# Rewriting the head statistics of an mLSTM stage, with a fourth raw weight tile and another order of loads and exponentials, in a two-layer streaming encoder

## The chip, the cores and the metric

The kernel runs on 1 core of a Trainium2 chip (trn2). The time is device microseconds of one execution on that core, the median of three runs. Besides, one execution was taken by the hardware profiler; every view of a profile below comes from that one. The engines are called PE (TensorE's matmuls; PEld is its weight loads), DVE (VectorE), ACT (ScalarE), POOL (GpSimd) and SP (SyncE, which only issues transfers here).

## The reference, cut to what matters

The program is an encoder trunk of two layers over 512 tokens of width 1024, in f32. Layer 0 mixes with 4 mLSTM heads of width 192 and 4 heads of attention to 256 memory tokens; layer 1 mixes with 12 heads of band attention and again memory attention. Each layer ends in a gated MLP with a causal convolution. What the change touches is the mLSTM head and what is done to its result:

```python
num = einsum('bhts,bhse->bhte', s, vv) + inter[..., None] * einsum('bhtd,bhde->bhte', qq, c_st)
den = sum(s, axis=-1) + inter * einsum('bhtd,bhd->bht', qq, n_st)
h = num / maximum(abs(den), exp(-m_t))[..., None]
...
hm = hm * rsqrt(mean(hm * hm, axis=-1, keepdims=True) + EPS)      # per head, 192 wide
mix_out = hm * a_head_g * sigmoid(o)
x = x + concatenate([mix_out, mem_out], axis=-1) @ w_out
```

The division by the bounded denominator and the norm of a head's row are one scale per token and head: with q = max(den², exp(-2 m)), the row `num` is multiplied by 1 / sqrt(mean(num²) + EPS q). Both versions of the kernel compute that.

## The kernel before

All activations lie transposed: 128 channels on the partitions, 512 tokens along the row. An f32 matrix is split into a rounded part and a rest, and a product is three matmuls (`mm3`, L167 to L171). A raw weight tile comes by SP's queue into one of three `wr` buffers (`load`), and ACT and DVE split it into `wh` and `wl` (`parts`, L130 and L131). `project` is one tile of 128 outputs over 8 such steps, with a yield behind each.

Order: a planner places the instructions on each engine by the order in which they are written and by its own estimate of when they are ready. The written order comes from generators: `weave(job, filler, each)` takes `each` steps of the filler for every yield of the job, and a yield of a number counts for that many. `pin` puts an instruction behind the one written before it on its engine. In the stage of this case the jobs are `mlstm_head(0)` to `mlstm_head(3)` and two rounds of memory attention, and the fillers are projections (query, key, gate and memory query tiles: `a_tiles`, `a_memory_queries`) and, later, parts of the output projection (`OutProjection.part`, which accumulates groups of output tiles over the input tiles that are there already; `finish` does the remaining output tiles whole and feeds the next norm).

A head: `weighted_scores(s)` for the four key tiles (an exponential of a row that POOL has spread over the partitions, L1155; a triangular mask on POOL, L1157; the scores in a PSUM bank, L164 and L519; their product on DVE, L1166; its split by ACT and DVE into `pt`), `products(s)` (two PSUM tiles `nums`, which hold 192 value channels, and the row sums spread over the 64 partitions that are left), then the statistics: both tiles squared on ACT (L1193) and multiplied by the output gate on DVE (L1195), and for each of four token tiles two f32 matmuls with the constants `mcf` as moving operand, which sum the squares of the numerator in one column and the mean of the squared denominators in the other:

```python
nc.tensor.matmul(st[:, 2 * T : 2 * T + 2], sqs[0][:, sl], mcf[:, 0, :], start=True, stop=False)
nc.tensor.matmul(st[:, 2 * T : 2 * T + 2], sqs[1][:, sl], mcf[:, 1 + odd, :], start=False, stop=True)
yield 0.581
```

The denominators are bounded from below by `floor2`, an exponential of the running maxima `mr`, which eight small transposes bring, with `acol`, to token-major columns (L1096 to L1099). Then come a reciprocal root by Newton's steps (`rsqrt`), two diagonal matrices (`diagonal`) and a matmul with ones (`spread`, L244) that brings the scale back along the rows, and the gated rows are scaled and split (L1214 to L1217) for the output projection. The memory's keys and values (`load_memory_kv`) come through a `wr` buffer. Buffers that matter: `u`, 57 tiles of 128x512; `bias`, 4 tiles for the spread exponents, asked for `NEXT` = 4 ahead; PSUM banks `mm` 3, `sc` 3, `tr` 2.

Of the kernel before, what the change touches and what calls it, by code (L numbers as in the profile page):

```python
# [55 lines left out]
def trunk(  # L56
# [25 lines left out]
    bufs = {"wr": 3, "wh": 3, "wl": 3, "u": 57, "t": 8, "pt": 2, "s": 16, "rb": 3, "bias": 4}  # L82
# [32 lines left out]

    mcf = cpool.tile([P, 3, 2], F32, name="mcf")
    V.memset(mcf, 0.0)
    V.memset(mcf[:, 0, 0:1], 1.0)
    V.memset(mcf[:HD, 1, 0:1], 1.0)
    V.memset(mcf[HD:, 1, 1:2], 1.0 / HD)  # L120
    V.memset(mcf[:HD, 2, 1:2], 1.0 / HD)
    V.memset(mcf[HD:, 2, 0:1], 1.0)

# [49 lines left out]
    def project(w, c0, act, tag="mm"):  # L173


        n = len(act)
        wh, wl = weights(rows(w, c0, P), n, P)
        o = ps(tag)
        for k in range(n):
            mm3(o, wh[:, k, :], wl[:, k, :], act[k][0], act[k][1], k == 0, k == n - 1)  # L180
            yield
        return o
# [374 lines left out]
    def memory_attention(q, kv, hp, mixes):  # L557
# [7 lines left out]
        def softmax(T2):  # L565
# [5 lines left out]
            for h in range(2):  # L571
# [3 lines left out]
                for i in range(2):  # L575
                    A.activation(e[:, i, :], ss[h][:, i, :], AF.Exp, bias=mx[:, i : i + 1], accum_out=sm[:, i : i + 1])
# [30 lines left out]
    class OutProjection:  # L607
# [19 lines left out]
        def finish(self, gnames):  # L627
            logarithms()
            norm = Norm()
            acts = [[] for _ in gnames]  # L630
            for j in range(KT):
                o = self.o[j] if j in self.o else run(project(self.w, j * P, self.mixes))
# [382 lines left out]
    floor2 = cpool.tile([P, TT, AH], F32, name="floor2")  # L1015
    NEXT = 4
# [14 lines left out]
    def gate_rows():  # L1031
# [19 lines left out]
        lfr, br, ar, mr = (sb("t", [P, S])[:AH, :] for _ in range(4))  # L1051
# [43 lines left out]
        for T in range(TT):  # L1095
            nc.tensor.transpose(tp[:, T * AH : (T + 1) * AH], ar[:, T * P : (T + 1) * P], ident[:AH, :AH])  # L1096
            nc.tensor.transpose(tp[:, 16 + T * AH : 16 + (T + 1) * AH], mr[:, T * P : (T + 1) * P], ident[:AH, :AH])
        pin(V.tensor_copy(acol, tp[:, :16].rearrange("p (t h) -> p t h", t=TT)))
        A.activation(floor2, tp[:, 16:32].rearrange("p (t h) -> p t h", t=TT), AF.Exp, scale=-2.0)  # L1099
# [3 lines left out]
    def qk_tile(c):  # L1103
# [8 lines left out]
        A.activation(acc, acc, AF.Silu)  # L1112
# [31 lines left out]
    def mlstm_head(h):  # L1144
# [6 lines left out]
        def weighted_scores(s):  # L1151
# [3 lines left out]
            A.activation(e[:, :n], spreads.pop((h, s)), AF.Exp, bias=acol[:, s, h : h + 1])  # L1155
# [34 lines left out]
        sqs = []  # L1190
        for o, j, r in ((nums[0], full, slice(0, P)), (nums[1], sh, rs)):
            sq = sb("t", [P, S])
            A.activation(sq, o, AF.Square)  # L1193
            sqs.append(sq)
            V.tensor_tensor(out=og[j][r, :], in0=o[r, :], in1=og[j][r, :], op=ALU.mult)  # L1195
        yield
        st = ps("sc")
        for T in range(TT):
            sl = slice(T * P, (T + 1) * P)
            nc.tensor.matmul(st[:, 2 * T : 2 * T + 2], sqs[0][:, sl], mcf[:, 0, :], start=True, stop=False)  # L1200
            nc.tensor.matmul(st[:, 2 * T : 2 * T + 2], sqs[1][:, sl], mcf[:, 1 + odd, :], start=False, stop=True)
            yield 0.581
        st = st[:, : 2 * TT].rearrange("p (t c) -> p t c", c=2)
        z, fc = small(), small()
        V.tensor_tensor(out=z, in0=st[:, :, 1], in1=floor2[:, :, h], op=ALU.max)
        V.tensor_scalar(z, z, EPS, 1e-35, op0=ALU.mult, op1=ALU.max)
        V.scalar_tensor_tensor(z, st[:, :, 0], 1.0 / DH, z, op0=ALU.mult, op1=ALU.add)
        rsqrt(fc, z)
        dg = diagonal(fc)
        yield 2.673  # L1210
# [8 lines left out]
    outp = OutProjection(a_w_out, mixes, (0, 3, "mm"), (3, 5, "tr"))  # L1219
# [5 lines left out]
    run(fill)  # L1225
    fill = chain(a_tiles(2), a_memory_queries(0), a_tiles(3, 4), a_tiles(5), a_memory_queries(1))
    memkv = load_memory_kv(0)
    weave(mlstm_head(0), fill, 1.4)
    until(lambda: og[2] is not None, fill)
    weave(mlstm_head(1), fill, 1.125)  # L1230
# [11 lines left out]
    fill = chain(fill, outp.part(1, 0, 1, 2, 6), outp.part(1, 3, 7))  # L1242
    weave(job, fill, 0.862)
    run(chain(fill, outp.part(0, 4, 5), outp.part(1, 4, 5)))
# [278 lines left out]
```

## Time and profile before

| | |
|---|---|
| median of 3 runs | 1194.93 us (1194.7 to 1196.32) |
| profiled execution | 1195.72 us |
| its span, first to last instruction | 1194.0 us |
| mean granted TensorE clock | 0.999 |
| PE busy | 1183.5 us (99%) |
| DVE busy | 961.7 us (81%) |
| ACT busy | 725.2 us (61%) |
| POOL busy | 130.3 us (11%) |
| head stage, about | 100 to 255 us of the span |

In a timeline row stand the start and the duration in us, the engine, the line of the kernel, the operation, output<-inputs by the program's names, the shapes and, in brackets, the idle time before it with what ended it. Matmuls overlap, so the time one takes of the engine is read from its start to the next one's. A row of a group has the busy time in us and the mean duration in ns behind the bar. A row of the waits has the sum in us, the number and the longest. A row of a window has its length and the busy time (and count) of PE, PEld, DVE, ACT and POOL, the granted clock, the DMA engines' share and GB/s. "f32" on PE stands for split operands too; an unsplit f32 matmul shows as two passes.

### The profile page before, as it was taken

The numbers are of one execution on the slowest core, as the hardware profiler recorded it, in microseconds if no ns is written. First come the engines' busy times: TensorE is split into PE (matmuls) and PEld (weight loads), VectorE is DVE, ScalarE is ACT, GpSimd is POOL, SyncE is SP. The second block draws the span as 40 slices with busy tenths as digits, with TensorE's granted clock in tenths as the row PEclk, the third lists the DMA queues.
The fourth block names the chain that finished last, engine by engine and source line by source line (L and its number), as shares of the span: only waits on it lengthen the run. The fifth ranks groups of instructions, "written<-read, shape, count | busy, mean of one in ns | idle before, by whom it ended". The sixth has DMA issues, their size and how long they took to land.

```text
span 1194.0 us, 18184 instructions
## 1 busy us (share of the span) xinstructions
PE 1183.5 (99%) x6719; PEld 1037.0 (87%) x6719; DVE 961.7 (81%) x1760; ACT 725.2 (61%) x1294; POOL 130.3 (11%) x222
## 2 busy tenths in 40 slices
PE   9999999999999999999999999999999999999997
PEld 9988888888899998999888888888889988999986
DVE  6877788788978888888698888997896888888855
ACT  5648677655656555555576677776565655555545
POOL 1211201010021111111020000101001011011100
PEclk9999999999999999999999999999999999999999
DMA  8645313444265676665464313246336455665551
GB/s 289 212 108 140 84 54 80 152 144 141 88 156 147 156 165 165 154 144 123 142 204 123 89 54 101 69 135 185 111 99 141 116 139 135 142 141 139 119 158 71
DMA packets 200155, 158.61 MB, mean 133 GB/s; under 512 B 8344, under 2 KB 179838, under 8 KB 200066
## 3 DMA queue, kind: packets, MB, share of 16 engines
q1 hardware_dynamic: 183906, 119.74, 34.1%
q0 software_dynamic: 15584, 36.67, 14.9%
q8 instruction: 53, 0.87, 0.3%
q10 hardware_dynamic: 576, 1.05, 0.2%
q14 instruction: 36, 0.29, 0.1%
HBM read 128.89 MB, written 32.46 MB: 135 GB/s over the span
## 4 chain that ended last, share of the span: by engine, by line
PE 92%; ACT 3%; DVE 2%; DMA 1%; SPq 1%; issue 0%; POOL 0%; POOLq 0%; DVEq 0%; ACTq 0%
PE pmm L169 15%; PE pmm L170 15%; PE pmm L171 15%; PE ptr L171 6%; PE ptr L169 6%; PE ptr L170 6%; PE pmm L785 6%; PE psc L171 5%; PE psc L170 5%; PE psc L169 5%; PE pmm L784 3%; PE psc L519 2%; PE ptr L1350 1%; DMA wr<-in_mem_w_kv_dram 1%; PE ptr L1371 1%; PE ptr L1372 1%
## 5 line engine op out<-in xcount | busy, mean ns | idle before, releaser
L169 PE MATMUL pmm<-u,wh 128*128 128x512 f32 (+1 forms) x872 | 309.1, 355 | 0.3 <-ACT u L130 0.2
L170 PE MATMUL pmm<-u,wh 128*128 128x512 f32 (+1 forms) x872 | 306.2, 351 | 0.0
L171 PE MATMUL pmm<-u,wl 128*128 128x512 f32 (+1 forms) x872 | 306.0, 351 | 0.0
L131 DVE TENSOR_TENSOR wl<-wr,wh 128x1024 fp32r<-128x1024 f32 (+3 forms) x172 | 199.8, 1163 | 57.0 <-ACT wh L130 55.0
L130 ACT CAST wh<-wr 128x1024 fp32r<-128x1024 f32 (+3 forms) x172 | 172.4, 1004 | 97.7 <-PE pmm L170 44.5
L171 PEld LDWEIGHTS pmm<-u,wl 128*128 128x128 f32 x872 | 164.5, 189 | 21.1
L169 PEld LDWEIGHTS pmm<-u,wh 128*128 128x128 f32 x872 | 164.5, 189 | 18.5 <-ACT u L130 1.1
L170 PEld LDWEIGHTS pmm<-u,wh 128*128 128x128 f32 x872 | 164.7, 189 | 18.2 <-DVE u L131 0.5
L169 PE MATMUL ptr<-u,wh 128*128 128x512 f32 x272 | 106.7, 392 | 0.0
L171 PE MATMUL ptr<-u,wl 128*128 128x512 f32 x272 | 106.1, 390 | 0.0
L753 POOL DMA_DIRECT2D xspill<-t x64 | 55.6, 869 | 461.1 <-ACT t L752 450.4
L170 PE MATMUL ptr<-u,wh 128*128 128x512 f32 x272 | 105.9, 389 | 0.0
L130 ACT CAST u<-pt 128x512 fp32r<-128x512 f32 x102 | 63.0, 620 | 46.8 <-DVE pt L875 46.7
L131 DVE TENSOR_TENSOR u<-pt,u 128x512 fp32r<-128x512 f32 x102 | 69.9, 688 | 11.2 <-ACT u L130 8.5
L169 PE MATMUL psc<-u,wh 128*128 128x256 f32 (+1 forms) x232 | 76.1, 328 | 0.0
L171 PE MATMUL psc<-u,wl 128*128 128x256 f32 (+1 forms) x232 | 75.9, 327 | 0.0
L170 PE MATMUL psc<-u,wh 128*128 128x256 f32 (+1 forms) x232 | 75.9, 327 | 0.0
L937 ACT ACTIVATE t<-t 128x512 f32<-128x512 f32 x34 | 21.6, 634 | 79.3 <-DVE t L660 79.3
L785 PE MATMUL pmm<-u,u 128*128 128x512 f32 x192 | 69.6, 397 | 0.0
L821 DVE TENSOR_TENSOR t<-t,pmm 128x256 f32<-128x256 f32 x72 | 30.2, 419 | 44.9 <-ACT t L819 44.8
L752 ACT COPY t<-ptr 128x512 f32<-128x512 f32 x64 | 37.4, 585 | 43.1 <-PE ptr L171 43.1
L660 DVE SCALAR_TENSOR_TENSOR t<-t,cols,t 128x511 f32<-128x511 f32 x80 | 59.7, 746 | 3.7 <-ACT t L667 3.7
(300 smaller groups left out, 2673.8 us busy)
## 6 DMA issues: line engine op xcount, KB each, us to landing
wr<-in_ffn_w_up_dram SPq DMA_DIRECT2D x54, 512.0 KB, 4.2
wr<-in_ffn_w_down_dram SPq DMA_DIRECT2D x38, 512.0 KB, 4.1
pt<-in_ffn_w_up_dram SPq DMA_DIRECT2D x34, 512.0 KB, 6.2
xspill<-t POOLq DMA_DIRECT2D x64, 256.0 KB, 5.2
wr<-in_a_w_in_dram SPq DMA_DIRECT2D x20, 512.0 KB, 3.7
xspill<-u POOLq DMA_DIRECT2D x32, 256.0 KB, 2.6
u<-xspill SPq DMA_DIRECT2D x32, 256.0 KB, 5.0
wr<-in_w_kv_dram SPq DMA_DIRECT2D x12, 512.0 KB, 3.7
```

Of the source, the lines that this page charges most:

```text
L130: high = A.copy(hi, src) if on_act else V.tensor_copy(hi, src)
L131: low = V.tensor_tensor(out=lo, in0=src, in1=f(hi), op=ALU.subtract)
L169: nc.tensor.matmul(o, lh, rh, start=first, stop=False, skip_group_check=more)
L170: nc.tensor.matmul(o, lh, rl, start=False, stop=False, skip_group_check=more)
L171: nc.tensor.matmul(o, ll, rh, start=False, stop=last, skip_group_check=more)
L519: nc.tensor.matmul(o, a, b, start=first and i == 0, stop=i == 1)
L660: V.scalar_tensor_tensor(acc[:, n:], src[:, : S - n], self.fw[:, c * FT + j : c * FT + j + 1], acc[:, n:], op0=ALU.mult, op1=ALU.add,)
L752: A.copy(t, o)
L753: G.dma_start(xspill[j], t, accum_op=ALU.add)
L784: nc.tensor.matmul(r[:, :H], w[1][:, k], p[i - 1][:, :H], start=False, stop=False, skip_group_check=True)
L785: nc.tensor.matmul(r, w[0][:, k], p[i - 1], start=False, stop=k == n - 1, skip_group_check=True)
L821: V.tensor_tensor(out=o, in0=o, in1=r[:, H:], op=ALU.add)
```

## The change

- The two squared tiles are combined before they are summed. The rows of the second tile that hold squared denominators are scaled and bounded by floors in one DVE operation, then both tiles are added (`tensor_add`), and one f32 matmul with a column of ones per token tile sums them, four per head. `mcf` and its six memsets go. The gate's multiplications are written behind the squares. The due times in the tail of a head become 3.6 and 5.
- The floors are rows now: `floor_rows` takes the exponential of `mr` (4 rows of 512), scales and bounds it, stores it in DRAM and loads each row back over 64 partitions, into two `u` tiles that live until the heads 1 and 3 have used them. Four of the eight small transposes go.
- `wr` has 4 buffers, `bias` 3, and `NEXT` is 3.
- `load_memory_kv(0)` is written behind head 0.
- The Silus of the query and key tiles, the exponentials of the heads' scores and those of memory attention (in both layers) are pinned.
- Output tile 5 becomes a third group of the first output projection, in an `sc` bank, whose parts over the inputs 0, 1, 2, 3, 6 and 7 are written into head 3's filler; `finish` (in both layers) loads and splits the weights of the first two tiles that remain before the norm's work.

```diff
-    bufs = {"wr": 3, "wh": 3, "wl": 3, "u": 57, "t": 8, "pt": 2, "s": 16, "rb": 3, "bias": 4}
+    bufs = {"wr": 4, "wh": 3, "wl": 3, "u": 57, "t": 8, "pt": 2, "s": 16, "rb": 3, "bias": 3}
...
-    mcf = cpool.tile([P, 3, 2], F32, name="mcf")
-    V.memset(mcf, 0.0)
...
-    def project(w, c0, act, tag="mm"):
+    def project(w, c0, act, tag="mm", ready=None):
...
-        wh, wl = weights(rows(w, c0, P), n, P)
+        wh, wl = ready or weights(rows(w, c0, P), n, P)
...
-                    A.activation(e[:, i, :], ss[h][:, i, :], AF.Exp, bias=mx[:, i : i + 1], accum_out=sm[:, i : i + 1])
+                    pin(
+                        A.activation(
+                            e[:, i, :], ss[h][:, i, :], AF.Exp, bias=mx[:, i : i + 1], accum_out=sm[:, i : i + 1]
+                        )
+                    )
...
             logarithms()
+            rest = [j for j in range(KT) if j not in self.o]
+            ready = {j: weights(rows(self.w, j * P, P), KT, P) for j in rest[:2]}
...
-                o = self.o[j] if j in self.o else run(project(self.w, j * P, self.mixes))
+                o = self.o[j] if j in self.o else run(project(self.w, j * P, self.mixes, ready=ready.get(j)))
...
-    floor2 = cpool.tile([P, TT, AH], F32, name="floor2")
-    NEXT = 4
+    floor2 = dram.tile([AH, S], F32, name="floor2")
+    floors = []
+    NEXT = 3
...
-        lfr, br, ar, mr = (sb("t", [P, S])[:AH, :] for _ in range(4))
+        lfr, br, ar = (sb("t", [P, S])[:AH, :] for _ in range(3))
+        mr = sb("rb", [P, S])[:AH, :]
+        floors.append(mr)
...
-            nc.tensor.transpose(tp[:, 16 + T * AH : 16 + (T + 1) * AH], mr[:, T * P : (T + 1) * P], ident[:AH, :AH])
         pin(V.tensor_copy(acol, tp[:, :16].rearrange("p (t h) -> p t h", t=TT)))
-        A.activation(floor2, tp[:, 16:32].rearrange("p (t h) -> p t h", t=TT), AF.Exp, scale=-2.0)
+
+    def floor_rows():
+        mr = floors.pop()
+        pin(A.activation(mr, mr, AF.Exp, scale=-2.0))
+        V.tensor_scalar(mr, mr, EPS * DH / HD, 1e-35, op0=ALU.mult, op1=ALU.max)
+        G.dma_start(floor2, mr)
+        for hp in range(2):
+            floors.append(sb("u", [P, S]))
+            for odd, half in enumerate(reversed(HEADS)):
+                row = floor2[2 * hp + odd]
+                src = bass.AP(tensor=row.tensor, offset=row.offset, ap=[[0, HD], [1, S]])
+                G.dma_start(floors[hp][half, :], src)
...
-        A.activation(acc, acc, AF.Silu)
+        pin(A.activation(acc, acc, AF.Silu))
...
-            A.activation(e[:, :n], spreads.pop((h, s)), AF.Exp, bias=acol[:, s, h : h + 1])
+            pin(A.activation(e[:, :n], spreads.pop((h, s)), AF.Exp, bias=acol[:, s, h : h + 1]))
...
         sqs = []
+        for o in reversed(nums):
+            sqs.insert(0, sb("t", [P, S]))
+            A.activation(sqs[0], o, AF.Square)
+        dr = HEADS[1 - odd]
+        V.scalar_tensor_tensor(
+            sqs[1][dr, :], sqs[1][dr, :], EPS * DH / HD, floors[hp][dr, :], op0=ALU.mult, op1=ALU.max
+        )
+        V.tensor_add(sqs[0], sqs[0], sqs[1])
         for o, j, r in ((nums[0], full, slice(0, P)), (nums[1], sh, rs)):
-            sq = sb("t", [P, S])
-            A.activation(sq, o, AF.Square)
-            sqs.append(sq)
             V.tensor_tensor(out=og[j][r, :], in0=o[r, :], in1=og[j][r, :], op=ALU.mult)
         yield
+        yield 3.6
         st = ps("sc")
         for T in range(TT):
-            sl = slice(T * P, (T + 1) * P)
-            nc.tensor.matmul(st[:, 2 * T : 2 * T + 2], sqs[0][:, sl], mcf[:, 0, :], start=True, stop=False)
-            nc.tensor.matmul(st[:, 2 * T : 2 * T + 2], sqs[1][:, sl], mcf[:, 1 + odd, :], start=False, stop=True)
-            yield 0.581
-        st = st[:, : 2 * TT].rearrange("p (t c) -> p t c", c=2)
+            nc.tensor.matmul(st[:, T : T + 1], sqs[0][:, T * P : (T + 1) * P], ones[:, :1], start=True, stop=True)
         z, fc = small(), small()
-        V.tensor_tensor(out=z, in0=st[:, :, 1], in1=floor2[:, :, h], op=ALU.max)
-        V.tensor_scalar(z, z, EPS, 1e-35, op0=ALU.mult, op1=ALU.max)
-        V.scalar_tensor_tensor(z, st[:, :, 0], 1.0 / DH, z, op0=ALU.mult, op1=ALU.add)
+        V.tensor_scalar(z, st[:, :TT], 1.0 / DH, None, op0=ALU.mult)
         rsqrt(fc, z)
         dg = diagonal(fc)
-        yield 2.673
+        yield 5
         fb = spread(dg, "sc")
...
-    outp = OutProjection(a_w_out, mixes, (0, 3, "mm"), (3, 5, "tr"))
+    outp = OutProjection(a_w_out, mixes, (0, 3, "mm"), (3, 5, "tr"), (5, 6, "sc"))
...
+    floor_rows()
     fill = chain(a_tiles(2), a_memory_queries(0), a_tiles(3, 4), a_tiles(5), a_memory_queries(1))
-    memkv = load_memory_kv(0)
     weave(mlstm_head(0), fill, 1.4)
     until(lambda: og[2] is not None, fill)
+    memkv = load_memory_kv(0)
...
-    fill = chain(fill, outp.part(1, 0, 1, 2, 6), outp.part(1, 3, 7))
+    fill = chain(fill, outp.part(2, 0, 1, 2, 3, 6, 7), outp.part(1, 0, 1, 2, 6), outp.part(1, 3, 7))
     weave(job, fill, 0.862)
-    run(chain(fill, outp.part(0, 4, 5), outp.part(1, 4, 5)))
+    run(chain(fill, outp.part(0, 4, 5), outp.part(1, 4, 5), outp.part(2, 4, 5)))
```

More of the change, by code (lines that the diff above doesn't have):

```diff
@@ L114, in trunk @@
     V.memset(eps, EPS)
-    mcf = cpool.tile([P, 3, 2], F32, name="mcf")
[L117 to L122, printed above, removed]
     HEADS = (slice(0, HD), slice(HD, P))
```

## The prediction

> **What bounds the kernel now.** I read the page first, then the waits of TensorE (PE), then the timeline of each engine through the stage of the four mLSTM heads, and last the table by windows. The page and the waits:
>
> ```profile
> span 1194.0 us, 18184 instructions
> PE 1183.5 (99%) x6719; PEld 1037.0 (87%) x6719; DVE 961.7 (81%) x1760; ACT 725.2 (61%) x1294; POOL 130.3 (11%) x222
> PE 92%; ACT 3%; DVE 2%; DMA 1%; SPq 1%; issue 0%; POOL 0%; POOLq 0%; DVEq 0%; ACTq 0%
> ...
> PE pmm L428 <- DVE mcf L117: 1.1, 1, 1.1
> PE ptr L392 <- ACT cols L320: 0.9, 1, 0.9
> PE ptr L588 <- DVE t L579: 0.3, 1, 0.3
> ```
>
> PE is busy for 1183.5 of 1194.0 us, 92% of the chain that ends last runs on it, and its longest visible wait after the start is 0.3 us. A transfer or another engine that gets faster therefore gives nothing by itself; what is taken out of PE's stream counts in full, if the stream stays dense. Busy time hides two things, though. Matmuls overlap, so a price has to be read from start to start; and a stall shorter than a matmul's tail shows only as a start that comes late. The timeline of PE around the statistics of head 0 shows the pace:
>
> ```profile
> 120.16 0.40 PE L170 MATMUL pmm<-u,wh 128*128 128x512 f32 x1
> 120.39 0.39 PE L171 MATMUL pmm<-u,wl 128*128 128x512 f32 x1
> 120.62 0.40 PE L169 MATMUL pmm<-u,wh 128*128 128x512 f32 x1
> ...
> 125.21 0.28 PE L1200 MATMUL psc<-mcf,t 128*128 128x2 f32 x2
> 125.35 0.36 PE L1201 MATMUL psc<-mcf,t 128*128 128x2 f32 x2
> 125.57 0.36 PE L1200 MATMUL psc<-mcf,t 128*128 128x2 f32 x2
> 125.80 0.36 PE L1201 MATMUL psc<-mcf,t 128*128 128x2 f32 x2
> 126.02 0.47 PE L169 MATMUL pmm<-u,wh 128*128 128x512 f32 x1
> 126.33 0.39 PE L170 MATMUL pmm<-u,wh 128*128 128x512 f32 x1
> ```
>
> A 512-column matmul takes 0.23 us (120.16, 120.39, 120.62). A statistics matmul moves two columns and still takes 0.11 us a pass: two passes from 125.57 to 125.80, and eight, two token tiles, 0.81 us from 125.21 to 126.02. The 512-column matmul behind such a burst is followed after 0.31 us (126.02 to 126.33), 0.08 us late.
>
> **The f32 sum (the largest term).** The groups by line, over the head stage:
>
> ```profile
> L1201 PE MATMUL psc<-mcf,t 128*128 128x2 f32 x32 | 5.8, 251 | 0.0
> L1200 PE MATMUL psc<-mcf,t 128*128 128x2 f32 x32 | 4.9, 222 | 0.0
> ```
>
> The 64 passes are 4 heads x 4 token tiles x 2 matmuls x 2 passes. By the rows above, the 16 tiles cost 8 x 0.81 = 6.5 us. In the timeline they stand in about three bursts a head with fill between, 12 in all, so 12 x 0.08 = 1.0 us of late starts come on top; and the first pair of a burst takes 0.14 us (125.21 to 125.35) instead of 0.23, which four bursts more than eight save, 0.4. Together 7.1 us. The new kernel has one matmul of one column per tile, 8 passes a head; that is the 0.81 us of the burst from 125.21 plus one late start, 0.9 us, and 3.6 us for four heads. Gain: 7.1 - 3.6 = **3.5 us**. Bounds: 0 if a new tile costs as much as the old pair; 7.1 - 4 x 0.81 + 4 x 0.14 = 4.4 if the new passes too are parted by fill and nothing behind them starts late. I take 3.5, since the row is of the same form but for a column. The Trainium skill (TensorE: Matmul & The Clock Gate, Back-to-back issue gap) gives 81 ns a matmul for a sustained stream of weight load and matmul at 128 columns; by that the 32 passes would be worth 2.6 us and the time 0.9 us more. The row has 0.11 us, and the measurement decides.
>
> **Floors as rows.** Four of eight transposes go:
>
> ```profile
> 88.35 0.22 PE L1096 MATMUL ptr<-ident,t 4*128 4x4 f32 x1
> ...
> 88.81 0.20 PE L1097 MATMUL ptr<-ident,t 4*128 4x4 f32 x1
> 88.94 0.50 PE L169 MATMUL pmm<-u,wh 128*128 128x512 f32 x1
> ```
>
> Eight take 0.59 us (88.35 to 88.94), so four less give **0.3 us**. In exchange POOL gets one store and four broadcasts; its own broadcasts take 0.55 us each, and it idles 14.22 us ahead of the first of head 0:
>
> ```profile
> 100.53 0.55 POOL L1029 DMA_DIRECT2D bias<-exponents  x1 [14.22 <-ACT t L1155]
> 106.75 0.58 ACT L1126 ACTIVATE u<-pmm 128x512 f32<-128x512 f32 x1
> ```
>
> That is 5 x 0.55 = 2.8 us of issue, plus the landing of the store. They are read only ahead of head 0's statistics (125.21), some 17 us behind the gate at 106.75 after which the floors' exponential runs, so I cost it at nothing; without that cover head 0's mask would come some 3 to 5 us late (it stands on POOL behind them).
>
> **Squares and DVE.** Each head loses two small operations (0.16 us each) and gains a 64-row and a 128-row pass over 512 columns:
>
> ```profile
> L1195 DVE TENSOR_TENSOR u<-ptr,u 128x512 f32<-128x512 f32 (+1 forms) x8 | 5.4, 686 | 5.0 <-ACT t L1193 4.9
> L539 DVE TENSOR_TENSOR t<-ptr,t 64x512 f32<-64x512 f32 x4 | 2.7, 682 | 0.8 <-ACT t L538 0.8
> L1205 DVE TENSOR_TENSOR s<-psc,floor 128x4 f32<-128x4 f32 x4 | 0.7, 163 | 2.6 <-PE psc L1201 2.6
> 160.00:190.00 30.00, 29.92 (x145) 24.68 (x144) 24.88 (x44) 27.45 (x48) 0.66 (x2) 1.00 0.22 64
> ```
>
> 0.68 + 0.69 - 2 x 0.16 = 1.05 us a head, 4.2 us in all. In the fullest window of the stage (last row: PE, weight loads, DVE, ACT) DVE has 24.88 of 30 us, so 1.05 fits; and the longer due times (3.6 and 5 instead of 0.581 each and 2.673) leave the planner more projections to put beside it. Cost 0, bounds 0 to 4.2. The multiplications by the output gate now follow the squares instead of standing between them.
>
> **Third group of the output projection.** After head 3 PE waits for its split rows:
>
> ```profile
> 251.75 0.39 PE L171 MATMUL ptr<-u,wl 128*128 128x512 f32 x1
> 252.30 0.96 PE L169 MATMUL pmm<-u,wh 128*128 128x512 f32 x3 [0.16 <-ACT u L130]
> 253.10 0.50 PE L170 MATMUL pmm<-u,wh 128*128 128x512 f32 x1
> 253.44 0.39 PE L171 MATMUL pmm<-u,wl 128*128 128x512 f32 x1
> ```
>
> 0.55 instead of 0.23 us from 251.75 to 252.30, 0.80 instead of 0.69 for the next three, 0.34 instead of 0.23 behind them: 0.5 us. The new group puts 6 x 3 matmuls, 18 x 0.23 = 4.1 us, ahead of that point: gain **0.5 us**. It is also the cover for the next part; the work itself is only moved out of the end of the block. The two weight tiles loaded ahead there find PE dense and change nothing.
>
> **Order of Silus and exponentials.** Pinning puts an instruction behind the one traced before it on its engine. A Silu already stands behind its own Identity; it stays. An exponential now stands behind the cast of the step before. Rows of head 3:
>
> ```profile
> 99.50 0.73 ACT L1155 ACTIVATE t<-bias,acol 128x512 f32<-128x512 f32 x1
> ...
> 230.53 0.73 ACT L1155 ACTIVATE t<-bias,acol 128x512 f32<-128x512 f32 x1
> 231.89 1.02 ACT L1155 ACTIVATE t<-bias,acol 128x384 f32<-128x384 f32 x2
> 232.82 0.60 ACT L130 CAST pt<-t 128x512 fp32r<-128x512 f32 x1
> 233.33 0.62 ACT L130 CAST u<-t 128x512 fp32r<-128x512 f32 x1
> ...
> 237.83 0.29 DVE L131 TENSOR_TENSOR pt<-t,pt 128x128 fp32r<-128x128 f32 x1 [0.37 <-ACT pt L130]
> ```
>
> Head 3's first exponential must follow the cast of the memory heads' result (233.33 + 0.62), 3.4 us later than 230.53. Exponential to cast is 2.9 us for the first step (230.53 to 233.42); I estimate 9.5 us for four steps of falling width, to 243.4 instead of 238.12: 5.3 us later. The statistics shrink from 1.8 to 0.9 us a head, the two passes more ahead of them take 1.4. So 0.5 of stall, 5.3 + 1.4 - 0.9 of delay and 4.1 of new cover leave a stall of up to 2.2 us, 1.7 worse than now, where I wrote a gain of 0.5. Between -1.7 and +0.5 I keep +0.5, since PE's stream has late starts of only some tenths in the same head where the exponentials are pressed most (0.43 us for a pass that takes 0.11):
>
> ```profile
> 233.04 0.28 PE L170 MATMUL psc<-u,u 128*128 128x128 f32 x1
> 233.47 0.73 PE L169 MATMUL ptr<-pt,u 128*128 128x512 f32 x2 [0.16 <-ACT pt L130]
> ```
>
> Such late starts come to about 1.4 us over the stage; that they go too is the bound below.
>
> Head 0's first exponential (99.50) must now follow the gate of tile 1 (106.75 + 0.58) and the floors' exponential, about 0.6 us: 107.9 instead of 99.5, 8.4 us later. Behind that stand three projections of tile 2, 3 x 24 x 0.23 = 16.6 us of PE work that needs nothing of head 0.
>
> **Fourth raw tile, three bias buffers, memory keys.** Casts wait for PE to free the split tiles, not for raw ones:
>
> ```profile
> L130 ACT CAST wh<-wr 128x1024 fp32r<-128x1024 f32 (+3 forms) x172 | 172.4, 1004 | 97.7 <-PE pmm L170 44.5
> ```
>
> So a fourth raw tile gives 0, on SP's queue an earlier issue. The spreads, three ahead instead of four, are asked for one head step later and paced more slowly: 0. The memory keys' casts only leave head 0 for head 1. The six memsets ahead of the first matmuls shift a start that waits for transfers: 0.
>
> **Sum.** 3.5 + 0.3 + 0.5 = 4.3 us. The profiled execution took 1195.72 us (span 1194.0), 0.8 above the median of the three runs, 1194.93; the gain is the same in both: 1195.72 - 4.3 = 1191.4, and by the median **1190.6 us**.
>
> **The rivals.** (a) DVE gives it back: the 4.2 us of passes fall on PE, 1190.6 + 4.2 = 1194.8, no change. For it: DVE 24.88 of 30 us. Against: PE's longest visible wait for DVE behind the start is 0.3 us. (b) Slower: the ordered exponentials starve PE. Head 0 starts 8.4 us late and, with POOL behind the floors, up to 4 more; head 3 ends with 2.2 us less than I took. It needs that the projections cannot come forward, because tiles are short:
>
> ```profile
> 142.51 1.10 POOL L499 MEMSET u<- 64x512 f32 x2 [0.91 <-PE psc L171]
> ```
>
> Here a memset waits for a tile that scores still hold, and the change holds two more such tiles through the heads. With 8.4 us exposed the time is 1190.6 + 8.4 = 1199.0; it decides from 4.3 + 2.4 = 6.7 us on. The same page of the Trainium skill (Architectural detail: the array is 16x 32x32, not 1x 128x128) says that ScalarE and VectorE take their queues strictly in order, so an exponential could not pass a cast that waits; the trace agrees in that no row shows one passing. (c) The change doesn't do what it says: one-column sums are issued in as many passes as before. Then 3.5 is gone: 1194.1.
>
> **How the numbers follow.** 0.2% is 2.4 us, about what a measurement of this kernel can tell from no change: faster is under 1192.5, slower over 1197.3. Forecast 0.63 (own range 1188.3 to 1192.4: 1190.6 less 1.4 of late starts and less 0.9 if the sums cost what their lower bound says, up to most of head 3's 2.2 lost), (a) 0.14, (c) 0.04, (b) 0.19. So faster 0.64 with a sliver of (a), same 0.17, slower 0.19. The range leaves out (b) and ends at (a) and (c) with the 1.4 us by which the highest run before lay over its median (1196.32): 1188.0 to 1196.5.
>
> **What would show it.** Right: the statistics' passes fall from 64 to 32 with 0.11 us each and bursts of 0.9 us a head; four transposes; no late start of over 0.1 us where the first group resumes after head 3; DVE about 4 us busier, PE's busy time about 4 us less. Wrong: late PE starts of 0.3 us and more in heads 0 or 3 behind ACT's casts or POOL's masks, DVE over 26 of 30 us in a window with PE waiting for it, or 64 passes still there.

## The result

The changed kernel takes **1202.51 us** (median of 6 runs, 1200.97 to 1203.48), the one before 1194.94 us: ratio 1.0060, 95% interval 1.0047 to 1.0072. It is slower by 7.6 us, where 4.3 us less were forecast. The profiled execution took 1200.97 us, its span 1199.3.

The page of the changed kernel, and what TensorE waited for:

```profile
span 1199.3 us, 18138 instructions
PE 1184.0 (99%) x6683; PEld 1032.2 (86%) x6683; DVE 965.6 (81%) x1756; ACT 720.1 (60%) x1291; POOL 132.9 (11%) x227
PE 78%; issue 9%; DVE 5%; ACT 5%; POOL 1%; DMA 1%; POOLq 0%; ACTq 0%; DVEq 0%
...
PE psc L160 <- ACT t L568: 3.5, 3, 2.2
...
PE psc L510 <- ACT t L568: 0.7, 2, 0.5
PE psc L1215 <- DVE t L1208: 0.6, 2, 0.4
```

PE's share of the chain falls from 92% to 78%. The longest wait is new: `psc`, the scores' bank, behind L568, the exponential of memory attention. (Lines are those of the changed kernel, up to ten less than before, and about ten more in the heads: L121 and L122 are the casts and splits, L160 to L162 `mm3`, L1165 the exponential of a head's scores, L1215 the sums. An edit of a run can shift them by a few.) Beside the starts in the trace of before, head 0's scale is spread 0.15 us later (134.09 before), head 1's 9.5 us (157.86), head 2's 7.9 (212.91), head 3's 8.1 (248.33). From the norm on everything is 4.9 us later, and at the end 5.4. So nearly all of the loss lies in the head stage. PE at the place, 180 to 190 us:

```profile
180.11 0.74 PE L510 MATMUL psc<-u,u 128*128 128x256 f32 x4 [0.49 <-ACT t L568]
180.70 0.70 PE L583 MATMUL ptr<-ident,t 128*128 128x128 f32 x4
183.58 0.50 PE L160 MATMUL psc<-u,u 128*128 128x512 f32 x1 [2.18 <-ACT t L568]
...
185.62 0.33 PE L162 MATMUL psc<-u,u 128*128 128x384 f32 x1
187.05 0.39 PE L160 MATMUL psc<-u,u 128*128 128x256 f32 x1 [1.10 <-ACT t L568]
```

Behind the first transposes of memory attention (180.70) stand head 2's scores, and no projection between. They need `sc` banks that memory attention's exponentials have yet to read, and ACT reads them late:

```profile
174.37 1.28 ACT L568 ACT_TABLE_LOAD   x1
175.67 0.47 ACT L568 ACTIVATE t<-psc,s 128x256 f32<-128x256 f32 x1
176.25 1.28 ACT L1122 ACT_TABLE_LOAD   x1
...
178.19 1.28 ACT L568 ACT_TABLE_LOAD   x1
179.49 0.47 ACT L568 ACTIVATE t<-psc,s 128x256 f32<-128x256 f32 x1
179.96 1.27 ACT L491 ACTIVATE u<-t 64x512 fp32r<-64x512 f32 x2
181.25 1.24 ACT L494 CAST u<-u 64x512 fp32r<-64x512 f32 x2
182.51 0.47 ACT L568 ACTIVATE t<-psc,s 128x256 f32<-128x256 f32 x1
```

Up to the third exponential ACT spends three table loads (3.8 us, one ahead of the first exponential) and the copies of the next queries (2.5 us, L491 and L494). That looked like the cause: pinned exponentials behind the copies. It is not, as the runs show.

### The profile page after: what moved, and what is told of

Its sections match the earlier page's. It is cut to its first block, busy times and chain, and to the rows that moved or that the text cites. A ratio compares the mean times of both kernels' runs of the same rounds, so it can differ in the third digit from the quotient of the medians.

```text
span 1199.3 us, 18138 instructions
## 1 busy us (share of the span) xinstructions
PE 1184.0 (99%) x6683; PEld 1032.2 (86%) x6683; DVE 965.6 (81%) x1756; ACT 720.1 (60%) x1291; POOL 132.9 (11%) x227
## 4 chain that ended last, share of the span: by engine, by line
PE 78%; issue 9%; DVE 5%; ACT 5%; POOL 1%; DMA 1%; POOLq 0%; ACTq 0%; DVEq 0%
PE pmm L160 11%; PE pmm L162 11%; PE pmm L161 11%; PE pmm L782 6%; PE ptr L160 5%; PE ptr L161 5%; PE ptr L162 5%; PE psc L160 4%; PE psc L162 4%; PE psc L161 4%; PE pmm L781 3%; PE psc L510 2%; PE ptr L1361 1%; DMA wr<-in_ffn_w_up_dram 1%; DVE u L122 1%
## 5 line engine op out<-in xcount | busy, mean ns | idle before, releaser
L160 PE MATMUL pmm<-u,wh 128*128 128x512 f32 (+1 forms) x864 | 305.3, 354 | 0.5 <-DVE t L1121 0.4
L162 PE MATMUL pmm<-u,wl 128*128 128x512 f32 (+1 forms) x864 | 303.2, 351 | 0.1
L161 PE MATMUL pmm<-u,wh 128*128 128x512 f32 (+1 forms) x864 | 303.2, 351 | 0.0
L122 DVE TENSOR_TENSOR wl<-wr,wh 128x1024 fp32r<-128x1024 f32 (+5 forms) x173 | 199.9, 1156 | 60.7 <-ACT wh L121 57.7
L121 ACT CAST wh<-wr 128x1024 fp32r<-128x1024 f32 (+5 forms) x173 | 172.4, 997 | 110.5 <-PE pmm L161 57.9
L162 PEld LDWEIGHTS pmm<-u,wl 128*128 128x128 f32 x864 | 163.0, 189 | 20.8 <-DVE wl L122 0.5
L160 PEld LDWEIGHTS pmm<-u,wh 128*128 128x128 f32 x864 | 163.0, 189 | 19.6 <-issue 0.8
L160 PE MATMUL ptr<-u,wh 128*128 128x512 f32 x272 | 106.5, 392 | 0.0
L162 PE MATMUL ptr<-u,wl 128*128 128x512 f32 x272 | 106.1, 390 | 0.0
L121 ACT CAST u<-pt 128x512 fp32r<-128x512 f32 x102 | 62.5, 616 | 46.2 <-DVE pt L872 46.1
L160 PE MATMUL psc<-u,wh 128*128 128x256 f32 (+1 forms) x240 | 79.4, 331 | 0.0
L162 PE MATMUL psc<-u,wl 128*128 128x256 f32 (+1 forms) x240 | 79.1, 329 | 0.0
L161 PE MATMUL psc<-u,wh 128*128 128x256 f32 (+1 forms) x240 | 79.0, 329 | 0.0
L122 DVE TENSOR_TENSOR u<-pt,u 128x512 fp32r<-128x512 f32 x102 | 69.9, 689 | 11.1 <-ACT u L121 8.5
```

Of the source, the lines that this page charges most:

```text
L121: high = A.copy(hi, src) if on_act else V.tensor_copy(hi, src)
L122: low = V.tensor_tensor(out=lo, in0=src, in1=f(hi), op=ALU.subtract)
L160: nc.tensor.matmul(o, lh, rh, start=first, stop=False, skip_group_check=more)
L161: nc.tensor.matmul(o, lh, rl, start=False, stop=False, skip_group_check=more)
L162: nc.tensor.matmul(o, ll, rh, start=False, stop=last, skip_group_check=more)
```

## Experiments

Ratios are against runs of the kernel before on the same chip (medians 1194.92 to 1195.36). A late start is the time by which a matmul starts later than the usual distance behind the one before it (the median for the same shapes in the same trace); sums of late starts leave out those under 0.05 us.

| version | median us | ratio, 95% interval |
|---|---|---|
| changed, no pins | 1194.18 | 0.9990 (0.9981 to 0.9999) |
| changed, memory attention not pinned | 1203.32 | 1.0070 (1.0055 to 1.0085) |
| changed, heads not pinned | 1194.38 | 0.9994 (0.9984 to 1.0003) |
| of the heads only head 1 pinned | 1197.56 | 1.0023 (1.0013 to 1.0033) |
| of the heads only head 1 not pinned | 1196.98 | 1.0010 (1.0000 to 1.0019) |
| changed, head 0 with less filler | 1205.36 | 1.0075 (1.0058 to 1.0091) |
| before with the pins alone | 1200.18 | 1.0036 (1.0023 to 1.0049) |
| changed without the due time of 3.6 | 1210.89 | 1.0129 (1.0112 to 1.0146) |
| before with the sums and floors alone | 1200.15 | 1.0036 (1.0024 to 1.0048) |
| no pins, keys ahead of head 0 | 1193.17 | 0.9983 (0.9974 to 0.9993) |
| the same with the buffers of before | 1198.54 | 1.0030 (1.0018 to 1.0042) |
| before with the other parts, 13 small tiles | 1205.59 | 1.0088 (1.0073 to 1.0103) |
| before with 13 small tiles | 1204.97 | 1.0084 (1.0067 to 1.0101) |
| before with the other parts, 12 small tiles | 1195.89 | 1.0008 (0.9999 to 1.0017) |
| no pins, keys ahead, spread due 6.5 | 1193.76 | 0.9984 (0.9974 to 0.9993) |
| no pins, keys ahead, sums due 5 | 1194.01 | 0.9984 (0.9974 to 0.9993) |

**First: pins, due time or sums.** Four runs, each with one part.

```diff
-        pin(A.activation(acc, acc, AF.Silu))
+        A.activation(acc, acc, AF.Silu)
...
-            pin(A.activation(e[:, :n], spreads.pop((h, s)), AF.Exp, bias=acol[:, s, h : h + 1]))
+            A.activation(e[:, :n], spreads.pop((h, s)), AF.Exp, bias=acol[:, s, h : h + 1])
```

> The changed kernel with no pin on the Silus and exponentials (heads, memory attention, floors); all else as changed. The profile of the changed kernel has about 7 us of PE stalls between 173 and 188 us, at the first memory attention, most of them a scores matmul that waits for a PSUM bank which exponentials (L568) have yet to read. Theory P (the pins made the exponentials late): the stalls go and the time falls from 1202.5 to about 1191 to 1195 us. Theory F (the longer due time of 3.6 per head uses filler up early and shifts which projection's casts fall between the exponentials): no change, 1201 to 1204 us. Theory K (the memory keys' casts behind head 0): no change.

Without the pins (the exponentials of memory attention and of the floors float as well) 1194.18 us: the pins cost 8.3 us here. What is left is 0.1% faster than before, not the 4.3 us of the forecast.

> The kernel before with the pins of the change alone (Silus, head exponentials, memory attention's exponentials). Theory P: stalls of 5 to 8 us at the first memory attention or in the heads, 1200 to 1204 us. Theories F and K: within 1 us of before, 1194 to 1196 us.

Those pins in the kernel before (all but the floors', which it hasn't): 1200.18 us, 5 us slower without the new sums. Theory P has the size here, but the loss isn't in one place: no start is over 0.7 us late, at memory attention none over 0.2. In the head stage the late starts come to 8.9 us where before has 4.5, and 1.6 us of that stand in a fall of the granted clock (last section).

```diff
-        yield 3.6
```

> The changed kernel without the line that yields 3.6 ahead of a head's sums, so that a head takes as many filler steps as before the change (the due time of 5 equals the old 4 x 0.581 + 2.673). Theory F: the stalls at the first memory attention go, 1191 to 1195 us. Theory P and theory K: no change, 1201 to 1204 us.

1210.89 us: without the due time the kernel is another 8.4 us slower, so the theory that the due time starves a later stage is wrong. It keeps PE from meeting the added squares and, above all, what stands behind them too early: without it a start of memory attention's scores is 3.0 us late behind head 1's scaled rows (165.37), and one of the output projection 2.3 us behind head 3's gated rows (254.71).

> The kernel before with the statistics of the change alone (floors as rows, added squares, one f32 sum per token tile, due times 3.6 and 5), nothing pinned, old buffers, old place of the memory keys, old output groups. If the sums are worth what the prediction's first term says, PE's 64 statistics passes become 32 and the time falls by about 3.5 us, to 1191 to 1192 us (theories P and K). Theory F: the 3.6 brings the stalls of the first memory attention with it, so 1197 to 1203 us.

1200.15 us: less work on PE, and 5 us slower. That was not expected by either theory, and the third group of runs is about it.

**Second: which pins.** One kind was left out at a time.

> The changed kernel, with memory attention's exponentials alone left floating (Silus, the heads' and the floors' exponentials stay in written order). Theory M, the fixed place of these 64 exponentials behind the queries' copies costs the 8.3 us that all the pins cost together: about 1195.5 us, and the two late starts of 2.4 and 1.3 us at 183 and 187 us are gone. Rival H, the heads' exponentials are what moves the interleaving: about 1201 us, and a stall of some us elsewhere in the same stage.

1203.32 us. Theory M is wrong: the planned order of PE stays the same, and so does the late start at the place.

> The changed kernel, with the heads' exponentials alone left floating (Silus, memory attention's and the floors' stay in order). Theory M: about 1200 us, with the 2.4 us late start behind memory attention's exponentials still there. Rival H: about 1195 us and no late start over 1 us.

1194.38 us: the heads' exponentials (L1165) carry the whole cost, 8.1 us. At the place, in this kernel:

```profile
175.47 0.60 PE L583 MATMUL ptr<-ident,t 128*128 128x128 f32 x4
175.83 0.48 PE L160 MATMUL pmm<-u,wh 128*128 128x512 f32 x1
...
180.45 0.39 PE L162 MATMUL pmm<-u,wl 128*128 128x512 f32 x1
180.68 0.39 PE L160 MATMUL psc<-u,u 128*128 128x512 f32 x1
```

The same transposes, the same scores, the same work on ACT (its three table loads stand at 168.72, 170.60 and 172.54, in the same order, and from the first of them to the third exponential it is 8.14 us in both), but between transposes and scores 18 projection matmuls, 4.1 us, and no late start. The kernel before has 15 there, the changed one none. ACT's chain isn't longer in the changed kernel; the work that hid it has gone elsewhere. Where to, the first exponential of head 1 shows, first in the changed kernel, then without the heads' pins:

```profile
136.47 1.21 ACT L121 CAST u<-u 128x512 fp32r<-128x512 f32 x2 [1.89 <-DVE u L1224]
137.59 1.26 ACT L500 CAST u<-wr 64x512 fp32r<-64x512 f32 x2
138.87 0.71 ACT L121 CAST u<-wr 128x256 fp32r<-128x256 f32 x2
139.61 1.28 ACT L1165 ACT_TABLE_LOAD   x1
140.90 0.72 ACT L1165 ACTIVATE t<-bias,acol 128x512 f32<-128x512 f32 x1
```

```profile
131.23 1.28 ACT L1165 ACT_TABLE_LOAD   x1
132.53 0.72 ACT L1165 ACTIVATE t<-bias,acol 128x512 f32<-128x512 f32 x1
...
138.04 1.25 ACT L500 CAST u<-wr 64x512 fp32r<-64x512 f32 x2
```

Pinned, it stands behind the cast of head 0's scaled rows, which waits for DVE until 136.47, and behind the casts of the memory's keys (137.59 to 139.58), and runs 8.4 us later. Floating, it runs ahead of both. The keys' casts are 2.0 us of that: in the kernel before with the pins alone, where the keys stand ahead of head 0, the same exponential is 6.5 us late (139.36 instead of 132.84). In the changed kernel the planner fills PE with projections meanwhile: 309 of their matmuls stand between the small transposes ahead of head 0 and memory attention's first, where the kernel without the heads' pins has 291; between the spreads of the heads 0 and 1 it is 99 instead of 82. Those 18 are missing behind the transposes. In the kernel before with the pins alone the planned order is another: 16 matmuls are left there, and it loses 5 us all the same. So the empty place is what the pins do in the changed kernel, not all that they can do.

```diff
+            if h in (1,):
+                pin(xp)
```

> The changed kernel with the exponentials of head 1 alone in written order among the heads' (Silus, memory attention's and the floors' as changed; heads 0, 2 and 3 floating). Theory C, head 1's late exponentials let the projections run ahead, so that none is left between memory attention's first transposes and head 2's scores: about 1201 us, no projection (at most 2 matmuls) in that place, and late starts of over 1 us there behind memory attention's exponentials. Rival S, it is the sum of delays in all four heads: about 1196.5 us (a quarter of the 8.1 us), and late starts spread over the stage.

1197.56 us, between the two expectations. In the planned order one projection is left at the place, and the late starts there are 0.9, 0.3 and 1.3 us, all behind memory attention; its profile has no fall of the clock. So theory C has the place right, and not the number: head 1 alone makes 3.2 of 8.1 us.

> The changed kernel with the exponentials of head 1 alone floating among the heads' (heads 0, 2 and 3, Silus, memory attention and floors in written order). Theory C, what the pins cost falls on the one place behind memory attention's first transposes, which head 1's order empties of projections: about 1195 us (1194.4 and some tenths), with no late start over 1 us between 170 and 190 us. Rival S2, the heads add up, 8.1 us less the 3.2 that head 1 alone cost: about 1199 us, with late starts in heads 0, 2 or 3.

1196.98 us: no late start over 0.3 us at the place, as theory C says, but 2.6 us dearer than without the heads' pins, so that C's number is missed again. More of it lies with the sums than anywhere else:

```profile
PE psc L1217 <- DVE t L1210: 1.4, 2, 0.8
```

In heads 1 and 2 they start 0.94 and 0.83 us late, behind the added squares; without the heads' pins it is 0.71 and under 0.3. The rest is several late starts of 0.4 to 0.7 us before products. 3.2 and 2.6 make 5.8 of 8.1 (by the ratios 3.5 and 1.9 of 7.9); the remainder comes only when both are together, and a part of it is the clock:

```profile
180.00:184.00 4.00, 1.57 (x9) 1.00 0.02 4
184.00:188.00 4.00, 3.26 (x14) 0.64 0.00 0
188.00:192.00 4.00, 4.00 (x15) 0.51 0.10 8
192.00:196.00 4.00, 4.00 (x20) 1.00 0.12 41
```

These are windows of the run without memory attention's pin, which has the changed kernel's order of all 6683 matmuls (length, PE busy, granted clock). Behind the late start of 2.3 us at 183.73 the clock falls to a half for some 7 us, and two matmuls in a row take 0.43 us instead of 0.23:

```profile
188.00 0.63 PE L160 MATMUL pmm<-u,wh 128*128 128x512 f32 x1
188.43 0.63 PE L161 MATMUL pmm<-u,wh 128*128 128x512 f32 x1
188.85 1.06 PE L579 MATMUL ptr<-ident,t 128*128 128x128 f32 x4
```

The profiled execution of the changed kernel itself had a clock of 1.00 there (mean 0.999, span 1199.3), the other five 0.996 to 0.997 and spans of 1200.6 to 1201.8: 1.3 to 2.5 us more, without a profile of their own. The profile without memory attention's pin, with the same order and the fall, has 0.996 and 1201.2 us, 1.9 more than the one without the fall; so that the other five had such a fall is likely, not shown. With head 1's pin alone, where no late start exceeds 1.3 us, the nine runs have 0.997 to 0.999.

```diff
-    weave(mlstm_head(0), fill, 1.4)
+    weave(mlstm_head(0), fill, 1.2)
```

> The changed kernel with all its pins, and head 0 taking 1.2 instead of 1.4 filler steps for each of its yields, so that more projections are left for memory attention (9 matmuls of 0.23 us, 2.1 us, between the first transposes and head 2's scores in the planned order, where the changed kernel has none and the one without the heads' pins 18). Theory C: the late starts of 2.4 and 1.3 us there shrink by some 2 us, and with no fall of the granted clock behind them the time is about 1198.5 us. Rival: the steps taken from head 0 are missed there, and the time is 1202 us or more, with late starts in head 0.

1205.36 us, a miss for theory C's number. The waits at the place shrink (1.9 us of late starts instead of 3.9), but a new one opens before it, 3.1 us long, with a fall of the clock behind it:

```profile
161.95 0.39 PE L162 MATMUL pmm<-u,wl 128*128 128x512 f32 x1
165.26 0.47 PE L160 MATMUL pmm<-u,wh 128*128 128x512 f32 x1 [2.92 <-DVE s L208]
```

With less filler for head 0 a projection stands where it waits for DVE. The row names a step of the reciprocal root (L208), which ended last; as that reads no bank, the release was more likely the operation before it, which reads a projection's bank until 165.11 (L1121, a tap of a key tile's convolution). The cover can't be dealt anew by one rate.

**Third: the sums by themselves, and the parts costed at nothing.**

> The changed kernel without any pin, and with the memory's keys and values loaded where the kernel before does it, ahead of head 0. Theory K, their loads, casts and splits ahead of head 0 are what made the statistics alone 6 us slower than the changed kernel without pins: about 1199 us, with a late start of 2 us in head 0 behind a cast. Rival B, the fourth weight tile and the third output group make that difference: 1194 to 1195 us, and head 0 as without pins (the spread of head 1 within 1 us).

1193.17 us: theory K is wrong, the keys' place costs nothing, ahead of head 0 it is 0.1% better if anything. It has the lowest median of all kernels here, 0.17% under the kernel before (interval 0.07 to 0.26%), and 0.8% under the changed one (0.9983 against 1.0060).

```diff
-    bufs = {"wr": 4, "wh": 3, "wl": 3, "u": 57, "t": 8, "pt": 2, "s": 16, "rb": 3, "bias": 3}
+    bufs = {"wr": 3, "wh": 3, "wl": 3, "u": 57, "t": 8, "pt": 2, "s": 16, "rb": 3, "bias": 4}
...
-    NEXT = 3
+    NEXT = 4
```

> The kernel without pins and with the memory's keys ahead of head 0 (1193.2 us), with the buffers of before: three raw weight tiles, four bias tiles, exponents four steps ahead. Theory W, the keys hold one of three raw tiles, the next projection's weights come 2 us late and a cast with them: about 1199 us and a late start of 2 us near 121 us of the span. Rival G, the third output group is what parts 1193.2 from 1200.2: 1193 to 1194.5 us.

1198.54 us: theory W holds, the buffers make 5.3 us beside the new sums, and G falls. ACT with three raw tiles, then with four:

```profile
116.17 0.51 ACT L121 CAST pt<-t 128x384 fp32r<-128x384 f32 x1 [1.22 <-DVE t L1172]
119.70 1.05 ACT L121 CAST wh<-wr 128x1024 fp32r<-128x1024 f32 x1 [3.01 <-DMA wr<-in_a_w_in_dram]
120.66 0.40 ACT L121 CAST pt<-t 128x256 fp32r<-128x256 f32 x1
```

```profile
111.86 1.05 ACT L121 CAST wh<-wr 128x1024 fp32r<-128x1024 f32 x1
114.12 0.51 ACT L121 CAST pt<-t 128x384 fp32r<-128x384 f32 x1 [1.22 <-DVE t L1172]
114.54 1.05 ACT L121 CAST wh<-wr 128x1024 fp32r<-128x1024 f32 x1
```

With three, a weight cast waits 3.01 us for its transfer. The keys hold one of the three raw tiles from their transfer at 85.98 to their casts from 111.48 on, and by the order of the issues the transfer that this cast waits for goes out only at 112.87, when DVE has left another. The casts of the head's scores queue up behind it, and PE's products with them:

```profile
124.26 0.39 PE L162 MATMUL pmm<-u,wl 128*128 128x512 f32 x1
126.81 0.33 PE L160 MATMUL ptr<-pt,u 128*128 128x128 f32 x1 [2.16 <-ACT pt L121]
```

With four, the transfer is there and the cast runs 0.4 us behind the one before it. The run with the sums alone has the same late start, 2.3 us at 123.61, with the clock at a half for 3.4 us behind it. The bias tiles and `NEXT` went with the raw tile, so the split between them is argued from the row, not run.

> The kernel before with its own sums, floors and floating exponentials, and the other parts of the change alone: fourth raw weight tile, three bias tiles and exponents three steps ahead, memory's keys behind head 0, third output group with its weights made ready (and 13 in place of 16 small tiles, since 24 of the words that held the constants of the sums are missing). Theory A, these parts win by themselves what they win beside the new sums (1200.2 to 1194.2): about 1189 us. Rival R, they only mend what the new sums upset: 1194 to 1195.5 us.

1205.59 us, outside both expectations. Head 3's spread is only 1.4 us later; the rest of the span is slower throughout, though no wait of PE there is longer and the granted clock is 0.999. The odd thing in that kernel was the 13 small tiles, so the next runs took that apart.

```diff
-    bufs = {"wr": 3, "wh": 3, "wl": 3, "u": 57, "t": 8, "pt": 2, "s": 16, "rb": 3, "bias": 4}
+    bufs = {"wr": 3, "wh": 3, "wl": 3, "u": 57, "t": 8, "pt": 2, "s": 13, "rb": 3, "bias": 4}
```

> The kernel before with 13 in place of 16 small tiles (of 128 bytes a partition) and nothing else changed. Theory L, the 384 bytes by which the tiles behind them move are what made the matmuls of 512 columns slower by some 4 ns each over the whole span in the run with the other parts alone: about 1203 us, and 230 to 232 ns from start to start where before shows 226 to 228. Rival T, too few small tiles or the other parts did it: 1195 us.

1204.97 us, with the matmuls in the very same order: theory L holds. Matmuls of 512 columns in the middle of the span, with 13 tiles and then in the kernel before:

```profile
399.78 0.40 PE L785 MATMUL pmm<-u,u 128*128 128x512 f32 x1
...
402.11 0.40 PE L169 MATMUL ptr<-u,wh 128*128 128x512 f32 x1
```

```profile
397.71 0.39 PE L169 MATMUL ptr<-u,wh 128*128 128x512 f32 x1
...
399.75 0.28 PE L169 MATMUL psc<-u,wh 128*128 128x256 f32 x1
```

Ten starts in 2.33 us (0.233 each) against nine in 2.04 (0.227).

> The other parts of the change alone beside the sums, floors and floating exponentials of before, as in the earlier run, but with 12 small tiles, so that the tiles behind them move by 512 bytes and not by 384. Theory L: the matmuls are back at 227 ns, and the time shows what these parts give by themselves: 1194 to 1197 us by the landmarks of the head stage (the third head's scale 1.4 us later than before). Rival T: about 1205 us again.

1195.89 us, as theory L has it. So the other parts by themselves give nothing (1.0008), and the new sums beside them take the ratio to 0.9990, some 2 us less.

**Fourth: what is left.**

> The kernel without pins and with the memory's keys ahead of head 0 (1193.2 us), with a due time of 6.5 instead of 5 between the sums and the spread of a head's scale. If the late starts of 0.35 and 0.30 us before the spreads of heads 0 and 1 (they wait for the diagonal matrices) are all that is moved: about 1192.5 us. If the projections that cover them are missed at memory attention, whose first transposes come 8 matmuls later by this: 1194 to 1196 us.

1193.76 us, in a profile with a span of 1191.5, the shortest of all; the late starts before the spreads are gone, but 0.3 us ones come up in memory attention. By median it is not parted from 1193.17.

> The same kernel (1193.2 us) with a due time of 5 instead of 3.6 ahead of the sums. If the wait of the sums for the added squares is what is left of the loss: about 1192.8 us (0.07 to 0.35 us of late starts are seen there). If the later sums push the chain of a head's scale into memory attention: 1194 to 1197 us.

1194.01 us: the sums wait no more, and 0.3 to 0.6 us come up at the spreads and at head 3's scores instead. Neither due time gets nearer to the forecast.

## Why the prediction was wrong

**The f32 sum: right in price.** The trace has 32 passes, and a head's eight take what the row of before promised:

```profile
126.92 0.95 PE L1215 MATMUL psc<-ones,t 128*128 128x1 f32 x8
127.73 0.49 PE L160 MATMUL pmm<-u,wh 128*128 128x512 f32 x1
128.05 0.40 PE L161 MATMUL pmm<-u,wh 128*128 128x512 f32 x1
```

0.81 us from 126.92 to 127.73 and a late start of 0.09 (kernel without the heads' pins), 0.9 a head. Over the stage the passes and the late starts behind them come to 7.1 us before (6.21, and 0.9 behind eleven bursts) and 3.7 here: 3.4 us, forecast 3.5. A pass takes 0.10 to 0.11 us; that decides over the 0.08 us that the Trainium skill (TensorE: Matmul & The Clock Gate, Back-to-back issue gap) gives at 128 columns. PE's busy time falls by 3.1 us without pins (1180.4). In the changed kernel it doesn't (1184.0); there a late start counts in part as busy, since the matmul before it overlaps nothing (2.34 us late at 183.58, 2.18 idle).

**Floors as rows: right.** Four transposes are left, and head 0 isn't late: its spread comes 0.15 us behind that of before, although its first exponential runs at 107.1 (forecast 107.9, before 99.5). So the cover held, for this head.

**Squares and DVE: the work right, the cost wrong.** DVE is 3.9 us busier (forecast 4.2), but 0 was too little. Without the heads' pins the sums of head 1 start 0.71 us late, and the spreads of heads 0 and 1 0.35 and 0.30:

```profile
153.62 0.39 PE L162 MATMUL pmm<-u,wl 128*128 128x512 f32 x1
154.56 1.05 PE L1215 MATMUL psc<-ones,t 128*128 128x1 f32 x8 [0.55 <-DVE t L1208]
```

That is 1.4 us, within the bounds of 0 to 4.2: rival (a) at a third of its price. The error was to test fit by an average over a window (24.88 of 30 us), where the question is when the chain of squares, bound and addition ends.

**Third group: right.** Without the heads' pins no late start over 0.11 us is left where the groups resume (0.54 us before). The run with the sums alone and the one with three raw tiles differ by this group and its ready weights alone: there the largest late start in head 3's tail falls from 0.84 (245.90) to 0.11 us. In the time that isn't parted (1.0036 and 1.0030).

**Order of the exponentials: the step that failed.** It was costed from the first exponential of head 0 and the end of head 3, with bounds of -1.7 to +0.5 us; head 0's cover held, and in head 3 no start is over 0.35 us late. The sum then put it at nothing and kept the third group's 0.5 us whole; the runs show a loss of 8.1 us for the heads' exponentials alone. In the changed kernel it lies first in head 1, whose first exponential is 8.4 us late behind the cast of head 0's scaled rows and the keys' casts, and in memory attention, neither of which was looked at. The cover was taken as there for whoever needs it; it is spent once, and the 18 matmuls that hide memory attention's table loads without the pins were spent ahead of it, 17 of them in head 1. Head 1's pin with this place makes 3.2 us, the pins of the other heads 2.6, by late sums and products; why both together cost 2.3 more is shown in part only (the clock). Nor did the working ask what the planner does with a head that it estimates as late.

**Fourth raw tile at 0: wrong beside the new sums.** With the bias tiles and `NEXT` it is worth 5.3 us there, which only keeps off a loss that the sums would bring with three tiles. "Casts wait for PE to free the split tiles, not for raw ones" was true of the kernel before as a sum over the span, and not of head 0 in the new order.

**Rivals.** (b) had the sign, 1199.0 us, and its cause, ordered exponentials that starve PE. Its place (heads 0 and 3) and its condition (projections that can't come forward for want of tiles) were wrong: they did come forward. The time went past the range's upper end, 1196.5, because (b) was left out of it, and past (b) itself. (c) is out, as the passes were halved. (The range's own sum gives 1188.3 to 1196.2 and not 1188.0 to 1196.5; nothing hangs on that.)

**The sum.** Of 4.3 us forecast, 0.8 to 1.1 are seen without the pins by median (1.8 by the profile's span). The gains came: 3.4 us from the sums, 0.25 from the transposes and 0.5 from the third group. What takes most of them back are new late starts, which the sum had at nothing: 1.4 us in the squares' chain, 0.55 and 0.53 us before the products of the heads 2 and 3 (0.33 in head 3 before), and many of a tenth. All late starts of the head stage come to 4.5 us before and 6.4 without the heads' pins, those behind the statistics' bursts included; in the changed kernel they come to 12.7.

## What to carry to other kernels

Fill work that hides a chain is a budget: when an order or a wait is changed, count for each later chain how many matmuls are still left between its first and its last step, in the planned order, instead of asking whether cover exists near the edit. To pin an instruction means to queue it behind everything written before, the end of the job before and the casts of another job included, so look at what those wait for and at what was moved ahead of it in the same change. A buffer that is idle on average can still be the one that decides under a new order: so look at how long a load sits in it.

## What the runs showed of the hardware

The granted clock fell to a half behind late starts of PE of some 2 to 3 us and stayed there for 3 to 7 us (0.51 in the window above, matmuls of 0.43 us), in most of the profiles with such a stall but not in all: of six with one of 2 us or more, four show it, and two, of the changed kernel (2.3 us) and of the one with three raw tiles (2.3), show 1.00 behind it. So a stall can cost more than its length. The Trainium skill (TensorE: Matmul & The Clock Gate, HAM oscillation — how this bites in real kernels) puts the limit at idle gaps over about 3.4 us; the half agrees, the limit doesn't, since a start 2.3 us late was enough. In the kernel before with the pins alone the clock fell with no late start over 0.7 us in the 15 us ahead of it:

```profile
246.00:248.00 2.00, 2.00 (x14) 0.90 0.00 0
248.00:250.00 2.00, 2.00 (x6) 0.50 0.05 15
```

What sets it off there is open.

Moving the tiles in SBUF by 384 bytes a partition (three small tiles less) slowed matmuls of 512 columns by some 2.5% from end to end and the kernel by 10 us, with no line of its work and no matmul's place in the order changed. A shift of 512 bytes, with one small tile less still, didn't; so it isn't the number of tiles. Which operand's address does it wasn't run.
